# Retention by chunks of 128 tokens with a carried state, in plain fp32, two heads to a PSUM tile

## The chip, the cores and the metric

One core of a Trainium2 chip runs the kernel. The metric is the device time of one execution in microseconds, and of several executions the median. Engines: TensorE (PE, its weight loads PEld), VectorE (DVE), ScalarE (ACT), GpSimd (POOL) and SyncE (SP), whose queue issues all DMAs here.

## What is computed

Two transformer layers over 512 latent and 256 context tokens of width 1024: modulated norm, an input projection, four mixers side by side (a convolution, two attentions of 4 heads, a retention of 4 heads), an output projection and an MLP. The second layer gives no output for the context. The change is in the retention, which runs forward and backward (on the flipped sequence), for each head with keys of 32 and values of 64:

```python
def retention_chunked(q, k, v, log_gamma, s0, with_output):
    ...
    k_decay = jnp.exp(lg * (RET_CHUNK - 1.0 - idx))
    chunk_kv = jnp.einsum('bhnjd,bhnje->bhnde', kc * k_decay[:, None, :, None], vc)
    chunk_decay = jnp.exp(log_gamma * RET_CHUNK)[:, None, None]

    def step(s, kv_j):
        return s * chunk_decay + kv_j, s

    s_final, s_prev = lax.scan(step, s0, jnp.moveaxis(chunk_kv, 2, 0))
    ...
    decay = jnp.where(diff >= 0, jnp.exp(lg[:, :, None] * jnp.maximum(diff, 0.0)), 0.0)
    scores = jnp.einsum('bhnid,bhnjd->bhnij', qc, kc) * decay[:, None]
    inner = jnp.einsum('bhnij,bhnje->bhnie', scores, vc)
    q_decay = jnp.exp(lg * (idx + 1.0))
    cross = jnp.einsum('bhnid,bhnde->bhnie', qc * q_decay[:, None, :, None], s_prev)
    return (inner + cross).reshape(b, h, l, dv), s_final
```

The latent pass starts from the final state of the context pass.

## The kernel before

Most products are made of three fp32r products (`mm3`): each operand is split into an fp32r part and an fp32r rest (`split`: a cast on DVE or ACT, a subtraction on DVE or POOL). Some products are plain fp32, which the profile shows as two records each.

No instruction is issued as it is written. `Plan.record` (L195) notes each operation with the engines that may do it and a cost; `VS`, `VG` and `VSG` are operations that may go to DVE or ACT, DVE or POOL, or any of the three, while `V`, `S`, `G`, `T`, `D` fix the engine. `Plan.schedule` (L384) then runs a list scheduler on these costs: an operation's priority is its place in the recorded program, buffers in SBUF and PSUM are given out as it goes, and a flexible operation goes to the engine that would end it first (`worse`, L514). `Plan.issue` (L642) emits the order that results, so nearly all instructions have line L645, and all buffers of SBUF have the name m in the trace, PSUM tiles b and pp. Each engine executes its own list in order.

`order_of` (L672) sets in which sequence the parts of `mixing` are recorded: projections and their preparation first, then attention units (a head with 256 query rows: scores, softmax, transposes, product with V), and among the last of them the retention: `ret_in` (L1425) once, then a piece of `s_ret` (L1490) after each further unit. At the end stand `s_read` (L1591: transposes, norm, gate) and `out_proj` (L1645), whose results `add_gated` (L1638) adds.

The retention before: `s_ret` takes one head at a time, latent (512 rows) and context (256 rows) apart. For each key tile t of 128 it multiplies K and Q (a stack of 96 rows that holds the three products of the split) for all queries of the segment, then for each direction d copies the needed columns of the scores to SBUF on ACT (`D_ = (3, 3)`: both directions in both layers), multiplies them by a table of decays `tabs[d]` on DVE or POOL, and multiplies V by the result into `op_[d]`. The columns are 512, 384, 256 and 128 wide for the four key tiles (256 and 128 in the context):

```python
                    op_ = [psG(nm="of"), psG(nm="ob")]
...
                            if D_[l] >> d & 1:
                                sc_ = smt([128, 512], nm="sc")
                                S.copy(out=sc_[:, 0:n], in_=s[:, a:b])
                                VG.tensor_tensor(out=Dt[:, 0:n], in0=sc_[:, 0:n], in1=tabs[d][:, o:o + n], op=ALU.mult)
```

`R = (15, 3)` has a bit for each head of a layer in which V and the masked scores are multiplied as plain fp32 (`whole`: all heads of layer 0, heads 0 and 1 of layer 1); the others are split. The context's state enters as one term (`state` times `qdec`) over all 512 latent rows.

Of the kernel before, what the change touches and what calls it, by code (L numbers as in the profile page):

```python
# [22 lines left out]
R = (15, 3)  # L23
# [27 lines left out]
D_ = (3, 3)  # L51
# [648 lines left out]
def block_kernel(ctx: ExitStack, tc: tile.TileContext, x, c, cx, c_ctx, w_mod, b_mod, w_in, w_out,  # L700
# [307 lines left out]
    def mixing(l, ht, yt, todo, late=None):  # L1008
# [414 lines left out]
        vr, QK, qdec, state, oT = {}, [], [], [], []  # L1423

        def ret_in():  # L1425
            for pr in PAIRS:
                if R[l] == 15 and pr != CTX:
                    continue
                vr[pr] = bigt([128, 2, 4, 2, 64], F32R, nm="vr")
                u4 = ur[pr][:, :, 256:512].rearrange("p i (h d) -> p i h d", h=4)  # L1430
                for i in range(2):
                    split(vr[pr][:, i, :, 0], vr[pr][:, i, :, 1], u4[:, i])
            for qk in range(2):
                hl = [bigt([128, 512 if last else 768], F32R, nm="rqk") for _ in range(2)]
                for a, ts in ((0, LAT), (512, CTX)):
# [9 lines left out]
                    if a == 0 and qk == 0:  # L1445
                        for d in range(2):
                            qt = smt([128, 512], nm="qt")
                            D.dma_start(out=qt, in_=qexp[d].partition_broadcast(128))
                            S.activation(out=qt, in_=qt, func=AF.Exp, scale=lgc[:, l, d:d + 1])
                            VG.tensor_tensor(out=qt, in0=qt, in1=kf, op=ALU.mult)  # L1450
                            qdec.append(bigt([128, 2, 512], F32R, nm="qdec"))
                            split(qdec[d][:, 0], qdec[d][:, 1], qt)
# [10 lines left out]
            uk_ = ur[CTX][:, :, 128:256].rearrange("p i (h e) -> p i h e", h=4)  # L1463
            for d in range(2):
                kd = smt([128, 2, 4, 32], nm="kdec")
                VG.tensor_tensor(out=kd, in0=uk_, in1=kdt[:, :, d].unsqueeze(3).to_broadcast([128, 2, 4, 32]), op=ALU.mult)
                kw_ = smt([128, 2, 256], F32R, nm="kdec2")
                split(kw_[:, 0], kw_[:, 1], kd.rearrange("p i h e -> p (i h e)"))
                p = psG((128, 4, 64), nm="state")
                mm3(p, [(kw_[:, 0, i * 128:(i + 1) * 128], kw_[:, 1, i * 128:(i + 1) * 128], vr[CTX][:, i, :, 0],  # L1470
                         vr[CTX][:, i, :, 1]) for i in range(2)])
                sm = smt([128, 4, 64], nm="sm")
                V.tensor_tensor(out=sm, in0=p, in1=own.unsqueeze(2).to_broadcast([128, 4, 64]), op=ALU.mult)
                ss_ = bigt([128, 4, 2, 64], F32R, nm="state")
                split(ss_[:, :, 0], ss_[:, :, 1], sm)
                state.append(ss_)
# [13 lines left out]
        def s_ret():  # L1490
            for h in range(4):
                whole = bool(R[l] >> h & 1)
                tabs = []
                for d in range(2):
                    di = smt([128, 512], nm="di")
                    D.dma_start(out=di, in_=dist[d])
                    S.activation(out=di, in_=di, func=AF.Exp, scale=lgam[:, l * 8 + d * 4 + h:l * 8 + d * 4 + h + 1])
                    if d == 0:
                        G.affine_select(out=di[:, 0:128], in_=di[:, 0:128], pattern=[[1, 128]], compare_op=ALU.is_ge,
                                        fill=0.0, base=0, channel_multiplier=-1)  # L1500
                    else:
                        G.affine_select(out=di[:, 384:512], in_=di[:, 384:512], pattern=[[-1, 128]], compare_op=ALU.is_ge,
                                        fill=0.0, base=0, channel_multiplier=1)
                    tabs.append(di)
                st3 = []
                for qk in range(2):
                    t3 = a3t([96, 512 if last else 768], F32R, nm="st3")
                    for blk, hl in enumerate(((0, 1, 0), (0, 0, 1))[qk]):
                        D.dma_start(out=t3[32 * blk:32 * blk + 32].bitcast(F32),
                                    in_=QK[qk][hl][32 * h:32 * h + 32].bitcast(F32))  # L1510
                    st3.append(t3)
                for seg in segs:
                    Q4, K4 = [t3[:, (0, 512)[seg]:(512, 768)[seg]] for t3 in st3]
                    if seg == 0:
                        nq = 512
                        order = [0, 1, 2, 3]
                    else:
                        nq = 256
                        order = [4, 5]

                    def rng(d, t):

                        jt = t if seg == 0 else t - 4
                        if d == 0:
                            return 128 * jt, nq, 0
                        return 0, 128 * (jt + 1), 384 - 128 * jt

                    def inner(d, t, first, end):
                        a, b, o = rng(d, t)
                        if whole:  # L1530
# [20 lines left out]
                    for t in order:  # L1551
# [19 lines left out]
                        if seg == 0:  # L1571
                            for d in range(2):
                                inner(d, t, False, t == order[-1])
# [329 lines left out]
```

## Time and profile before

| | us |
|---|---|
| median of 3 runs (1842.2 to 1846.6) | 1844.59 |
| the profiled execution, its own time | 1847.59 |
| its span | 1845.9 |
| PE busy | 1706.8 (92%) |
| PEld busy | 1403.2 (76%) |
| DVE busy | 1355.0 (73%) |
| ACT busy | 684.3 (37%) |
| POOL busy | 394.6 (21%) |

The mixing of layer 0 lies at some 50 to 490 us, its projection and MLP until some 1100, the mixing of layer 1 until some 1450, its projection and MLP from there to the end. The mean granted clock of TensorE was 0.958 of full speed. Ends of matmuls are modelled, so PE's busy time is not PE at its peak. A row of a form gives the count, busy us, the mean ns of one, and the engine's idle time before them with what ended it.

### The profile page before, as it was taken

How to read it: one execution, taken by the hardware profiler on the slowest of the kernel's cores; microseconds unless marked ns; L12 is line 12 of the kernel's file. 1: busy time of each engine (PE TensorE's matmuls, PEld its weight loads, DVE VectorE, ACT ScalarE, POOL GpSimd, SP SyncE). 2: the span in 40 equal slices, each digit the busy share in tenths (PEclk: the TensorE clock that was granted, in tenths of full speed). 3: DMA queues.
4: the chain of work that ended last, by engine and by line, in shares of the span. 5: the costliest groups of instructions: out<-in, count | busy, mean ns of one | idle time of the engine just before them, and what ended most of it. 6: DMA issues, size and time to landing. Idle time of an engine off the chain costs nothing. (4 is left out here: it accounts for less than half of the span.)

```text
span 1845.9 us, 23213 instructions
## 1 busy us (share of the span) xinstructions
PE 1706.8 (92%) x8587; PEld 1403.2 (76%) x8587; DVE 1355.0 (73%) x2309; ACT 684.3 (37%) x1257; POOL 394.6 (21%) x358
## 2 busy tenths in 40 slices
PE   6995789989999999999999999959897989999998
PEld 4784568656788877888888889748765878888886
DVE  6889448888896788676765577974988776666665
ACT  5522027977443112111211135213997342222222
POOL 3318013651510010100100021120433421000001
PEclk9998799989999999999999999969997999999999
DMA  9220031534241434424421212110121533333331
GB/s 304 67 75 12 0 97 49 173 111 133 69 138 46 137 99 130 133 88 146 158 70 47 86 36 75 47 52 12 34 60 61 167 95 100 110 96 92 103 91 58
DMA packets 140641, 168.67 MB, mean 91 GB/s; under 512 B 7658, under 2 KB 93274, under 8 KB 140528
## 3 DMA queue, kind: packets, MB, share of 16 engines
q1 hardware_dynamic: 140528, 167.20, 29.5%
q8 instruction: 67, 1.10, 0.2%
q14 instruction: 46, 0.38, 0.1%
HBM read 161.14 MB, written 2.10 MB: 88 GB/s over the span
## 5 line engine op out<-in xcount | busy, mean ns | idle before, releaser
L645 PE MATMUL b<-m,m 128*128 128x512 f32 (+5 forms) x6452 | 1366.8, 370 | 49.6 <-DVE m L645 40.7
L645 PEld LDWEIGHTS b<-m,m 128*128 128x128 f32 (+2 forms) x6452 | 1123.2, 191 | 263.4 <-DVE m L645 39.4
L645 DVE TENSOR_TENSOR m<-m,m 128x512 fp32r<-128x512 f32 (+8 forms) x665 | 548.9, 844 | 138.0 <-PE b L645 79.9
L645 ACT CAST m<-m 128x1024 fp32r<-128x1024 f32 (+6 forms) x354 | 278.8, 808 | 666.2 <-PE b L645 462.8
L645 POOL TENSOR_TENSOR m<-m,m 128x1024 fp32r<-128x1024 f32 (+11 forms) x158 | 274.7, 1750 | 1087.7 <-ACT m L645 571.4
L645 DVE TENSOR_TENSOR m<-b,m 128x512 f32<-128x512 f32 (+12 forms) x346 | 208.6, 611 | 124.3 <-PE b L645 108.6
L645 PE MATMUL pp<-m,m 128*128 128x512 f32 (+6 forms) x848 | 206.0, 369 | 18.9 <-DVE m L645 9.7
L645 PEld LDWEIGHTS pp<-m,m 128*128 128x128 f32 (+2 forms) x848 | 148.1, 197 | 56.0 <-ACT m L645 15.8
L645 PE MATMUL b<-ident,m 128*128 128x128 f32 (+4 forms) x730 | 111.2, 280 | 27.5 <-DVE m L645 24.0
L645 ACT COPY m<-b 128x512 f32<-128x512 f32 (+7 forms) x176 | 82.8, 491 | 126.6 <-PE b L645 120.4
L645 DVE TENSOR_TENSOR m<-m 128x256 f32<-128x256 f32 (+1 forms) x104 | 63.4, 611 | 82.9 <-ACT m L645 82.4
L645 PEld LDWEIGHTS b<-ident,m 128*128 128x128 f32 (+4 forms) x730 | 84.7, 141 | 48.7 <-DVE m L645 28.2
L645 DVE SCALAR_TENSOR_TENSOR m<-m,sf,m 128x1024 f32<-128x1024 f32 x80 | 102.9, 1298 | 24.3 <-DMA m<-in_w_mod_dram 24.2
L645 DVE CAST m<-m 128x512 fp32r<-128x512 f32 (+4 forms) x163 | 77.8, 481 | 56.3 <-PE pp L645 31.7
L645 ACT ACTIVATE m<-b 128x512 f32<-128x512 f32 (+1 forms) x115 | 60.6, 529 | 149.0 <-PE b L645 140.6
L645 DVE SCALAR_TENSOR_TENSOR m<-m,cvw,m 128x783 f32<-128x783 f32 (+1 forms) x120 | 100.7, 887 | 0.6
L645 DVE TENSOR_REDUCE ty<-pp 128x1 f32<-128x768 f32 (+1 forms) x66 | 60.8, 932 | 9.2 <-PE pp L645 8.6
L645 ACT ACTIVATE m<-m 128x1024 f32<-128x1024 f32 (+4 forms) x65 | 42.0, 650 | 52.5 <-DVE m L645 42.9
L645 ACT ACTIVATE m<-pp,ty 128x768 f32<-128x768 f32 (+1 forms) x66 | 58.5, 888 | 4.4 <-PE b L645 3.0
L645 POOL TENSOR_TENSOR ty<-ty,mhalf 128x1 f32<-128x1 f32 (+4 forms) x47 | 57.3, 1225 | 2.3
L645 PE MATMUL pp<-ident,m 128*128 128x128 f32 (+3 forms) x252 | 41.6, 287 | 13.4 <-ACT m L645 7.5
L645 POOL TENSOR_SCALAR ty<-ty 128x2 f32<-128x2 f32 (+4 forms) x43 | 16.3, 380 | 166.3 <-ACT m L645 107.3
(112 smaller groups left out, 669.4 us busy)
## 6 DMA issues: line engine op xcount, KB each, us to landing
m<-in_mlp_w_dram SPq DMA_DIRECT2D x128, 512.0 KB
m<-in_w_mod_dram SPq DMA_DIRECT2D x96, 512.0 KB
m<-in_w_in_dram SPq DMA_DIRECT2D x32, 512.0 KB
m<-in_w_out_dram SPq DMA_DIRECT2D x16, 512.0 KB
m<-in_x_dram SPq DMA_DIRECT2D x8, 512.0 KB
m<-in_dist_dram SPq DMA_DIRECT2D x16, 256.0 KB
m<-in_w_in_dram SPq DMA_DIRECT2D x8, 416.0 KB
m<-m SPq DMA_DIRECT2D x24, 96.0 KB
```

The source lines that it names most:

```text
L645: op.fn(*[f(a) for a in op.args], **{k: f(a) for k, a in op.kw.items()})
```

## The change

`s_ret` now takes two heads, e = 0 and 1, and only the diagonal blocks of 128 by 128 of the latent scores: four 128-column products into one PSUM tile, one mask product for each direction, on DVE and straight from PSUM. What earlier chunks contribute comes from four states for each direction, which `ret_in` builds in a chain (context, then each chunk: decay K, multiply with V, keep each head's own block, multiply the last state by `g128` and add). V lies in `vz` with zeros beside it, so that each product writes all 128 rows of a tile of two heads and both heads add up in one PSUM tile; one eviction then serves two heads. The context segment keeps its full 256 columns. All these products are plain fp32; only the scores stay fp32r. The decay tables are 128 columns wide (256 in layer 0), and their exponents are loaded once for a layer. `order_of` is the same, but `s_ret` has 2 pieces where it had 8 and 4.

```diff
-            for pr in PAIRS:
-                if R[l] == 15 and pr != CTX:
-                    continue
-                vr[pr] = bigt([128, 2, 4, 2, 64], F32R, nm="vr")
+            for pr in opairs:
+                vz[pr] = bigt([128, 2, 4, 2, 64], nm="vz")
+                G.memset(vz[pr], 0.0)
                 u4 = ur[pr][:, :, 256:512].rearrange("p i (h d) -> p i h d", h=4)
-                for i in range(2):
-                    split(vr[pr][:, i, :, 0], vr[pr][:, i, :, 1], u4[:, i])
+                for k in range(2):
+                    VSG.copy(out=vz[pr][:, :, k::2, k], in_=u4[:, :, k::2])
...
-                            qt = smt([128, 512], nm="qt")
-                            D.dma_start(out=qt, in_=qexp[d].partition_broadcast(128))
+                            qt = smt([128, 128], nm="qt")
+                            D.dma_start(out=qt, in_=qexp[d, 384 * d:384 * d + 128].partition_broadcast(128))
                             S.activation(out=qt, in_=qt, func=AF.Exp, scale=lgc[:, l, d:d + 1])
-                            VG.tensor_tensor(out=qt, in0=qt, in1=kf, op=ALU.mult)
-                            qdec.append(bigt([128, 2, 512], F32R, nm="qdec"))
-                            split(qdec[d][:, 0], qdec[d][:, 1], qt)
+                            qdec.append(bigt([128, 512], nm="qdec"))
+                            VG.tensor_tensor(out=qdec[d].rearrange("p (c n) -> p c n", c=4),
+                                             in0=kf.rearrange("p (c n) -> p c n", c=4),
+                                             in1=qt.unsqueeze(1).to_broadcast([128, 4, 128]), op=ALU.mult)
...
+            g128 = cst([128, 2], f"g128{l}")
+            S.activation(out=g128, in_=lgc[:, l], func=AF.Exp, scale=128.0)
             for d in range(2):
...
+                for n in range(4):
...
+                        t = n - 1 if d == 0 else 4 - n
+                        kd = smt([128, 4, 32], nm="kdec")
+                        VG.tensor_tensor(out=kd, in0=tile_of(ur, t)[:, 128:256].rearrange("p (h e) -> p h e", h=4),
+                                         in1=kdt[:, 1 - d, d].unsqueeze(2).to_broadcast([128, 4, 32]), op=ALU.mult)
+                        items = [(kd, tile_of(ur, t)[:, 256:512])]
+                    p = psG((128, 4, 64), nm="state")
+                    for i, (a, b) in enumerate(items):
+                        T.matmul(p.rearrange("p h e -> p (h e)"), lhsT=a.rearrange("p h e -> p (h e)"), rhs=b,
+                                 start=i == 0, stop=i == len(items) - 1)
+                    st = bigt([128, 4, 64], nm="state")
+                    V.tensor_tensor(out=st, in0=p, in1=own.unsqueeze(2).to_broadcast([128, 4, 64]), op=ALU.mult)
+                    if n:
+                        V.scalar_tensor_tensor(out=st, in0=states[d][-1], scalar=g128[:, d:d + 1], in1=st,
+                                               op0=ALU.mult, op1=ALU.add)
+                    states[d].append(st)
...
         def s_ret():
-            for h in range(4):
...
+            tw = 128 if last else 256
+            di = [wkt([128, tw], nm="dist") for _ in range(2)]
+            D.dma_start(out=di[0], in_=dist[0, :, 0:tw])
+            D.dma_start(out=di[1], in_=dist[1, :, 512 - tw:512])
+            for e in range(2):
+                dts = []
+                for h in (2 * e, 2 * e + 1):
...
+                    s = psG(nm="sT")
+                    for c in range(4):
+                        cs = slice(c * 128, (c + 1) * 128)
+                        T.matmul(s[:, cs], lhsT=K3[:, cs], rhs=Q3[:, cs], start=True, stop=True)
+                    for d in range(2):
+                        dt = smt([128, 4, 128], nm="Dt")
+                        V.tensor_tensor(out=dt, in0=s.rearrange("p (c n) -> p c n", c=4),
+                                        in1=tabs[d][1].unsqueeze(1).to_broadcast([128, 4, 128]), op=ALU.mult)
+                        for c in range(4):
+                            dts.append((d, 0, h, c, c * 128, c * 128 + 128, dt[:, c]))
...
+                    for d in range(2):
+                        dt = smt([128, 384], nm="Dc")
+                        V.tensor_tensor(out=dt[:, 0:256], in0=s[:, d], in1=tabs[d][0], op=ALU.mult)
+                        V.tensor_tensor(out=dt[:, 256:384], in0=s[:, 1 - d, 128 - 128 * d:256 - 128 * d], in1=tabs[d][1],
+                                        op=ALU.mult)
...
                 for seg in segs:
...
+                    for d in range(2):
+                        o = psG(nm="oret")
                         if seg == 0:
...
+                            for c in range(4):
+                                cs = slice(c * 128, (c + 1) * 128)
+                                T.matmul(o[:, cs], lhsT=states[d][c][:, 2 * e:2 * e + 2].rearrange("p h e -> p (h e)"),
+                                         rhs=qdec[d][:, cs], start=c == 0, stop=False)
+                        mine = [x for x in dts if x[0] == d and x[1] == seg]
+                        for i, (_, _, h, t, a, b, m) in enumerate(mine):
+                            T.matmul(o[:, a:b], lhsT=tile_of(vz, t)[:, h].rearrange("p k e -> p (k e)"), rhs=m,
+                                     start=seg == 1 and i == 0, stop=i == len(mine) - 1)
+                        VS.copy(out=oT[d][e][seg], in_=o[:, 0:(512, 256)[seg]])
+                yield
```

The change also moves what the planner makes of the rest. Over the whole program PE has 7207 rows before and 7198 now, DVE 2124 and 2073, ACT 1103 and 1010, POOL 335 and 320, SP 415 and 404 (a row is an instruction or several equal ones in a row). Two places of it follow.

ACT in layer 0, before, in the middle of the retention (b and pp are PSUM tiles, m buffers of SBUF; copies of 512, 384, 256 and 128 columns are scores):

```order
L645 ACTIVATE m_7303,ty_3580<-b_3587,ty_3581 128x256
L645 CAST m_7316<-pp_7299 128x512
L645 COPY m_6627<-b_3587 128x512
L645 CAST m_7333<-pp_7300 128x512
L645 COPY m_7246<-b_3587 128x128
L645 COPY m_7137<-pp_7327 128x384
L645 COPY m_6627<-pp_7327 128x256
L645 COPY m_7351<-b_3586 128x256
L645 COPY m_7246<-b_3586 128x384
L645 COPY m_7355<-b_3587 128x128
```

and now, where the retention's tables are made (lgam holds the logarithms of the decays) and the softmax goes on:

```order
L643 ACTIVATE m_6305<-m_6227,lgam 128x256
L643 ACTIVATE m_6227<-m_6305,lgam 128x256
L643 CAST m_6777<-b_3426 64x256
L643 ACTIVATE m_3492<-m_6227,lgam 128x256
L643 ACTIVATE m_6784<-m_6305,lgam 128x256
L643 ACTIVATE m_6540<-m_6227,lgam 128x256
L643 ACTIVATE m_6540<-m_6305,lgam 128x256
L643 CAST m_5879<-pp_6678 64x512 x2
L643 COPY m_6589<-b_3424 64x256
L643 ACTIVATE m_6305,ty_3408<-pp_6903,ty_3407 128x768
L643 ACTIVATE m_6305<-m_6305,ty_3404 128x768
```

The copies of scores are gone from ACT, and six of the eight tables stand close together, each 256 wide.

DVE at the end of the mixing of layer 1, before (a reduction to 128x1 from pp is a softmax, one to 128x8 from m is the readout of the retention, the additions 64x512 and 64x256 from PSUM the last evictions of attention and retention):

```order
L645 TENSOR_REDUCE ty_3573<-pp_15551 128x1
L645 TENSOR_TENSOR m_15569<-m_15222,m_15333 128x1024
L645 TENSOR_TENSOR m_14879<-b_3588,m_14887 64x512
L645 RECIPROCAL ty_3564<-ty_3567 128x1
L645 TENSOR_TENSOR m_14879<-b_3585,m_14879 64x256
L645 TENSOR_TENSOR m_14929<-m_14879,m_14917 64x256
L645 TENSOR_TENSOR m_15616<-m_15264,m_15519 128x1024
L645 CAST m_15641<-m_14879 128x512
...
L645 TENSOR_REDUCE ty_3569<-m_14379 128x8
L645 TENSOR_REDUCE ty_3574<-m_14379 128x8
L645 TENSOR_REDUCE ty_3566<-m_14423 128x8
```

and now:

```order
L643 TENSOR_REDUCE ty_3410<-pp_15059 128x1
L643 TENSOR_TENSOR m_14198<-b_3427,ty_3404 128x512
L643 TENSOR_REDUCE ty_3408<-m_15017 128x8
L643 TENSOR_REDUCE ty_3403<-m_14023 128x8
L643 RECIPROCAL ty_3421<-ty_3413 128x1
L643 TENSOR_TENSOR m_14198<-pp_14947,m_14198 64x256
L643 TENSOR_TENSOR m_14023<-pp_14948,ty_3415 128x512
L643 TENSOR_REDUCE ty_3423<-pp_15107 128x1
```

The readout's reductions stood behind the last softmax; now the last two of its four, and with them all four, stand ahead of it.

## Rows read from the trace of the kernel before

**Rows 1.** Windows; columns PE, PEld, DVE, ACT, POOL busy, clock, DMA, GB/s.

```profile
285.00:380.00 95.00, 90.17 (x578) 69.89 (x577) 88.11 (x180) 86.64 (x173) 55.92 (x38) 0.98 0.41 128
380.00:490.00 110.00, 103.33 (x512) 68.49 (x512) 90.79 (x187) 74.78 (x165) 45.06 (x52) 0.92 0.32 99
850.00:900.00 50.00, 50.00 (x249) 42.46 (x248) 35.81 (x47) 7.32 (x10) 4.81 (x4) 1.00 0.31 97
1290.00:1390.00 100.00, 89.01 (x532) 68.89 (x531) 91.24 (x195) 92.49 (x198) 38.89 (x39) 0.98 0.20 59
1390.00:1448.00 58.00, 46.12 (x220) 36.97 (x219) 47.99 (x84) 36.35 (x66) 28.99 (x24) 0.82 0.18 64
```

**Rows 2.** Waits of DVE and ACT (380 to 490), PE (1390 to 1448): us, times, longest.

```profile
DVE m L645 <- PE b L645: 3.9, 5, 1.4
...
ACT m L645 <- PE b L645: 20.1, 14, 6.7
...
ACT m L645 <- DMA m<-in_dist_dram: 0.3, 1, 0.3
...
PE b L645 <- DVE m L645: 8.2, 5, 2.9
```

**Rows 3.** PE timeline in 403 to 414 and 1102 to 1104, one group by form.

```profile
405.34 0.43 PE L645 MATMUL pp<-m,m 128*64 128x128 f32 x2
407.84 0.65 PE L645 MATMUL b<-m,m 128*64 128x256 f32 x2
411.05 3.04 PE L645 MATMUL b<-m,m 128*128 128x256 f32 x20
...
1102.52 1.45 PE L645 MATMUL pp<-m,m 128*128 128x160 f32 x6
...
L645 PE MATMUL b<-m,m 128*128 128x512 f32 x4607 | 1072.2, 392 | 21.1 <-DVE m L645 13.5 <-ACT m L645 6.0 <-DVE modc L645 1.5
```

**Rows 4.** Groups by form on DVE, ACT and POOL, whole span.

```profile
L645 DVE TENSOR_TENSOR m<-m,m 128x512 f32<-128x512 f32 x191 | 143.6, 756 | 7.3 <-PE b L645 1.7 <-ACT m L645 0.7
L645 DVE TENSOR_TENSOR m<-m,m 128x384 f32<-128x384 f32 x20 | 13.1, 656 | 2.8 <-PE pp L645 1.5 <-PE b L645 1.0 <-ACT m L645 0.3
L645 DVE TENSOR_TENSOR m<-m,m 128x256 f32<-128x256 f32 x21 | 8.9, 440 | 1.4 <-POOL m L645 1.1 <-PE b L645 0.3
L645 DVE TENSOR_TENSOR m<-m,m 128x128 f32<-128x128 f32 x22 | 7.3, 337 | 0.2
L645 DVE TENSOR_TENSOR m<-b,m 128x512 f32<-128x512 f32 x180 | 122.8, 687 | 107.4 <-PE b L645 105.7
L645 DVE CAST m<-m 128x512 fp32r<-128x512 f32 x98 | 44.3, 455 | 5.0 <-ACT m L645 2.3 <-PE b L645 0.3
L645 DVE SCALAR_TENSOR_TENSOR m<-m,cvw,m 128x512 f32<-128x512 f32 x60 | 41.9, 746 | 0.3
L645 ACT COPY m<-b 128x512 f32<-128x512 f32 x78 | 44.5, 593 | 91.9 <-PE b L645 91.1 <-PE pp L645 0.4
L645 ACT COPY m<-b 128x384 f32<-128x384 f32 x17 | 8.4, 493 | 7.2 <-PE b L645 7.2
L645 ACT COPY m<-b 128x256 f32<-128x256 f32 x20 | 7.6, 378 | 10.5 <-PE b L645 9.1 <-DVE m L645 1.2
L645 ACT COPY m<-b 128x128 f32<-128x128 f32 x13 | 3.5, 280 | 0.0
L645 ACT ACTIVATE m<-m,lgam 128x512 f32<-128x512 f32 x16 | 11.1, 722 | 0.4 <-DMA m<-in_dist_dram 0.3
L645 ACT ACTIVATE m<-m 128x256 f32<-128x256 f32 x12 | 5.0, 416 | 0.2
L645 ACT ACTIVATE m<-m 128x128 f32<-128x128 f32 x14 | 4.2, 303 | 0.1
L645 POOL MEMSET m<- 128x1024 f32 x10 | 9.3, 952 | 50.2 <-issue 28.2 <-DVE m L645 14.3 <-PE b L645 7.6
```

**Rows 5.** Group by form on DVE in 380 to 490.

```profile
L645 DVE TENSOR_TENSOR m<-b,own 128x256 f32<-128x256 f32 x1 | 0.4, 414 | 0.0
```

More of the change, by code (lines that the diff above doesn't have):

```diff
@@ L22 @@
 F = (0, 0)
-R = (15, 3)
 Q = (1, 1)
@@ L50 @@
 J = (0, 7)
-D_ = (3, 3)
 NCUT = 2
@@ L1420, in mixing @@
                 units.append(Unit(gqa_prep(h, pr, whole), h, 4, 2, pr, whole))
-        vr, QK, qdec, state, oT = {}, [], [], [], []
+        vz, QK, qdec, states, oT = {}, [], [], [[], []], []
         def ret_in():
-            for pr in PAIRS:
-                if R[l] == 15 and pr != CTX:
-                    continue
-                vr[pr] = bigt([128, 2, 4, 2, 64], F32R, nm="vr")
+            for pr in opairs:
+                vz[pr] = bigt([128, 2, 4, 2, 64], nm="vz")
+                G.memset(vz[pr], 0.0)
                 u4 = ur[pr][:, :, 256:512].rearrange("p i (h d) -> p i h d", h=4)
-                for i in range(2):
-                    split(vr[pr][:, i, :, 0], vr[pr][:, i, :, 1], u4[:, i])
+                for k in range(2):
+                    VSG.copy(out=vz[pr][:, :, k::2, k], in_=u4[:, :, k::2])
             for qk in range(2):
@@ L1462, in ret_in @@
             V.tensor_scalar(out=kdt, in0=kdt, scalar1=32.0 ** -0.5, scalar2=None, op0=ALU.mult)
-            uk_ = ur[CTX][:, :, 128:256].rearrange("p i (h e) -> p i h e", h=4)
+            g128 = cst([128, 2], f"g128{l}")
+            S.activation(out=g128, in_=lgc[:, l], func=AF.Exp, scale=128.0)
             for d in range(2):
[L1465 to L1476, printed above, removed]
@@ new lines, in ret_in @@
+                for n in range(4):
+                    if n == 0:
+                        kd = smt([128, 2, 4, 32], nm="kdec")
+                        uk_ = ur[CTX][:, :, 128:256].rearrange("p i (h e) -> p i h e", h=4)
+                        VG.tensor_tensor(out=kd, in0=uk_, in1=kdt[:, :, d].unsqueeze(3).to_broadcast([128, 2, 4, 32]),
+                                         op=ALU.mult)
+                        items = [(kd[:, i], ur[CTX][:, i, 256:512]) for i in range(2)]
+                    else:
+                        t = n - 1 if d == 0 else 4 - n
[13 more added lines that the diff above has]
+                    states[d].append(st)
@@ L1477, in ret_in @@
+            states[1].reverse()
             oT.extend([[[bigt([128, (512, 256)[s]], nm="oT") for s in segs] for _ in range(2)] for _ in range(2)])
```

116 lines of the change are left out of this document (25 added, 91 removed).

## The prediction

> **What bounds the kernel now.** I read the stages first, in the view of windows [rows 1]. In the MLP of layer 0 (850 to 900) PE is busy all 50 us and the two other engines idle a good part: there PE is the bound. In the mixing it is the other way round. In 285 to 380 DVE is busy 88.11 of 95 us and ACT 86.64; in 1290 to 1390 it is 91.24 and 92.49 of 100. PE looks busy there too (90.17, 89.01), but its ends are modelled, its weight loads fill only 70% of the time, and in the last stretch, 1390 to 1448, it falls to 46.12 of 58 with a granted clock of 0.82. The retention runs in 380 to 490 and 1390 to 1448, where DVE still does 90.79 of 110 and 47.99 of 58.
>
> Then the waits [rows 2]. In 380 to 490 ACT waits 20.1 us for PE; DVE idles 19.2 us in all (110 less 90.79), in small waits of which 3.9 us are for PE; and in 1390 to 1448 PE waits 8.2 us for DVE. So in the mixing DVE and ACT hand work to each other in a nearly full pipeline, and PE follows. The question is what the change takes from DVE and ACT, and the PE saving comes second.
>
> **PE.** A plain fp32 product is two records, and alone takes 0.43 us for 128 and 0.65 us for 256 columns [rows 3], so some 0.21 us for each block of 128 columns in a chain. Before, a head needs 26 such blocks in layer 0 (20 latent, 6 context); now 14, and 4 for its share of the carried states: 8 blocks less, 32 in all, 6.8 us. The three-product cross terms also go: 24 products of 512 columns at 0.23 us (busy over count in [rows 3]: 1072.2 us for 4607), 5.5 us. The carried states add 20 blocks against 12 narrow products: 2.8 us more. The scores fall from 16 products of 512 to 16 of 128 columns. No row shows that shape. A 160-column fp32r product takes 0.24 us (1.45 us for 6), more than a 256-column one (3.04 us for 20, 0.15 us); below, a quarter of 0.23 is 0.06. I take 0.21, the nearer row, so the scores save next to nothing. Sum for layer 0: about 9.5 us less; for layer 1, without context rows and with the two split heads, about 5. The Trainium skill, "FP8 and Floating Point Precision", "TensorE Precision Notes", separates reduced fp32 from true fp32 with its four passes; by a single pass in proportion to columns the scores would cost 0.06 us each and PE would save 2.4 us a layer more. The 160-column row speaks against it. The time hardly depends on it, since PE is not what ends the waits here.
>
> **DVE, ACT and POOL, which carry the sum** (durations from [rows 4] unless said).
> Removed in layer 0:
> - Score copies on ACT: per head and direction 512, 384, 256, 128 columns latent and 256, 128 context, at 0.593, 0.493, 0.378 and 0.280 us: 4.81 us a head, **19.2 us**.
> - Mask products on DVE or POOL at 0.756, 0.656, 0.44 and 0.337 us: **23.7 us**.
> - Evictions of half-height outputs, 8 at 0.593 and 8 at 0.378: 7.8 us. Tables, 8 exponentials at 0.722: 5.8 us.
> - Decayed queries, 2 times 0.722 + 0.756 + 0.455 + 0.756: 5.4 us. Context V, decayed K and states: 6 pairs of a cast (0.455) and a 256-wide product (0.44), and 4 single products: 7.1 us.
> Sum: 69 us.
> Added in layer 0:
> - Mask products straight from PSUM, on DVE alone: per head 2 of 512 at 0.687, and 2 of 256 and 2 of 128 at an estimated 0.42 and 0.28 (the 512 row scaled, a fixed part kept): **11.1 us**.
> - Tables at 0.416: 3.3 us. Evictions, half as many at full height: 3.9 us. Padded V: 3 fills at 0.952 on POOL and 6 copies at the cast's 0.455: 5.6 us. Decayed queries, an exponential at 0.303 and a product at 0.756 twice: 2.1 us.
> - State chain: 8 decays of K (2 at 0.44, 6 at 0.337), 8 masks by owner at 0.414 [rows 5], 6 multiply-adds. The form of the last is absent; between a 256-wide product (0.44) and a 512-wide multiply-add (0.746) I take 0.5. Together 9.2 us.
> Sum: 35 us. **Net 34 us less** on three engines.
> Layer 1 in the same way, with latent rows only: copies 14.0, masks 17.5, evictions 7.5, tables 5.8, the hi/lo split of the masked scores of heads 2 and 3 and of all V 18.7 (4 times 1.14 of cast, by columns, and 2.19 of subtraction; 6 pairs), the rest 10.8: 74 us; added 25 (masks 5.5). **Net 49 us less.** Some flexible operations move between engines, so what matters is what the plan gives each. In the new order ACT has 93 rows fewer, DVE 51, POOL 15. Adding up DVE's instructions of each order at the durations of their forms, up to the first gated addition of the output projection, DVE loses only 5 us in layer 0 but some 22 in layer 1; most of layer 0's relief is ACT's and POOL's.
>
> DMA: 16 loads of 256 KB for the distance tables become 4 smaller ones, and the SP queue gets shorter. ACT waited 0.3 us for them [rows 2], so I count nothing. The queue positions of the projection weights hardly move.
>
> **What of it reaches the time.** If DVE alone bounds the stage, layer 0 gains 5 us and layer 1 22. If the relief is shared evenly by DVE and ACT, 17 and 24. Layer 0: I take 10, since DVE's 19.2 us of idle time [rows 1] sit in the retention and shrink when a score needs one hop fewer. Layer 1: I take 21, near the DVE end, because DVE was full through 1290 to 1390. There the plan also puts the readout ahead of the last softmax, so its products are not left for the tail. What is late next is that last softmax chain in layer 1, and the PE-bound projection in layer 0. Sum 31 us. The profiled execution took 1847.59 us (span 1845.9), so 1816.6; the median of the runs is 3.0 below it, so **1813.6 us**.
>
> **Rivals.**
> - *Even sharing, and the clock recovers.* ACT's relief counts as much as DVE's: 17 + 24 = 41, and the low clock in 1390 to 1448 (0.82, so PE lost up to 10 us there) goes in part: 46 us, 1798.6. For it: ACT as full as DVE in 285 to 380. Against: the DVE count of layer 0.
> - *Only the fixed chain counts.* The order was made for costs that differ from the measured ones, and new waits open where DVE must read scores from PSUM: layer 0 gains nothing, layer 1 half (11): 1834. For it: DVE idles 17% of 380 to 490 though work is at hand on every engine.
> - *The clock falls.* Where PE does less, the granted clock was lower: 0.92 and 0.82 against 1.00 in the MLP [rows 1]. The Trainium skill, "TensorE: Matmul & The Clock Gate", Part 1, says that activity opens the clock and idling closes it between 1.2 and 2.4 GHz; the two rows agree. As a mechanism here: 0.08 of 110 and 0.18 of 58 us of clock missing mean 18 and 21 us at half rate, 39 us, which cost PE 19 us of work. Were the half-rate time doubled by thinner PE work, 19 of the 31 us come back: 1833.
> - *DVE stands behind PSUM (slower).* The mask products are now DVE's alone and stand in its in-order queue behind score matmuls; softmax reductions queue behind them. ACT took that wait before: 20.1 us in 14 waits, 1.4 us each [rows 2]. There are 24 such products in layer 0 and 8 in layer 1; at 1.4 us each, 46 us minus 31 gained: 15 slower, 1860. It decides above 1.0 us a product. Against: DVE's own waits for PE are 3.9 us in 5 times there, 0.8 us each, and the planner puts other ready work in between.
> - *It does not reach the time.* All that goes was hidden under PE, as PE's 94% in 380 to 490 would have it: 1844.6. Against: PE waits for DVE.
>
> **How the numbers follow.** Forecast (gain 24 to 38) 0.56; even sharing 0.13; only the chain 0.15; clock 0.07; DVE behind PSUM 0.05; no effect 0.04. The range reaches from the even-sharing case to the two smaller gains, with 1 us of spread between runs at either end (1842.2 to 1846.6 before): 1798 to 1835. No change means within 0.2%, 3.7 us, about what a measurement can tell. Faster 0.91, same 0.04, slower 0.05.
>
> **What would show it.** Right: in the mixing windows ACT's share falls clearly below DVE's; layer 1's mixing ends some 20 us earlier relative to its start, layer 0's some 10; the MLP stretches keep their length; PE has about 15 us less work; 128-column scores show 0.2 us each. Wrong: DVE idle behind PE in the retention (the slower rival), granted clock under 0.8 over the whole retention, or a layer 0 that gains as much as layer 1.

## The result, and the profile after

The changed kernel takes 1796.67 us (median of 4 executions, 1796.0 to 1801.06), beside 1843.39 us (1838.34 to 1846.6) for the kernel before in the same comparison: ratio 0.9754, 95% interval 0.9726 to 0.9782. That is 46.7 us less, where 31 were forecast; 1796.67 lies 1.3 us below the low end of the range. The profiled execution took 1797.3 us. One execution of the kernel before, in a later comparison, ran in a slow state (3408 us) and is left out of every figure.

The first part of the profile of the changed kernel, busy time and share of the span:

```profile
span 1795.6 us, 23051 instructions
PE 1662.4 (93%) x8623; PEld 1395.0 (78%) x8623; DVE 1321.9 (74%) x2257; ACT 641.6 (36%) x1166; POOL 377.8 (21%) x338
```

Against the table of before, DVE lost 33 us, ACT 43, POOL 17 and PE 44. The windows that answer to [rows 1], moved by the shift of their stage (columns as there):

```profile
282.00:377.00 95.00, 91.81 (x590) 70.64 (x589) 86.52 (x185) 87.85 (x179) 56.34 (x40) 0.98 0.38 116
377.00:476.00 99.00, 87.22 (x546) 74.05 (x544) 83.83 (x178) 57.38 (x117) 39.98 (x39) 0.97 0.34 105
834.00:884.00 50.00, 50.00 (x248) 42.36 (x247) 36.15 (x47) 7.32 (x10) 4.88 (x4) 1.00 0.33 100
1267.00:1367.00 100.00, 89.51 (x625) 77.90 (x624) 95.85 (x196) 88.50 (x181) 39.20 (x41) 1.00 0.20 56
1367.00:1401.00 34.00, 31.82 (x175) 26.37 (x174) 28.77 (x49) 19.64 (x38) 19.48 (x16) 1.00 0.30 99
```

Layer 0's first stretch and the MLP are as they were. In its retention (377 to 476) ACT fell from 68% to 58% of the window while DVE stayed at 83 to 85%. In layer 1 DVE is fuller than before (95.85 of 100 against 91.24), the granted clock is 1.00 to the end, and the thin stretch at the end (PE 46.12 of 58 us, clock 0.82) is now 34 us long with PE busy for 31.82. The waits that answer to [rows 2], in 377 to 476 (engine, what it waited for: us, times, longest):

```profile
ACT m L643 <- PE b L643: 20.5, 13, 4.5
...
DVE m L643 <- PE b L643: 3.2, 1, 3.2
```

They are much as they were. With the waits of the softmax reductions and for PE's other tiles counted, DVE waited 11.8 us for PE (9.5 in 380 to 490 before): it does not stand behind PSUM, although it now reads all scores there.

To see each layer whole, the span is cut at the first softmax reduction of each layer. But for a few preparations, both pieces hold the same parts of the program in every kernel: the first is layer 0's mixing with its MLP and the change of layers, the second is layer 1 from there to the end. The two windows before:

```profile
177.80:1203.70 1025.90, 974.94 (x4988) 802.42 (x4988) 753.34 (x1273) 357.93 (x674) 190.09 (x180) 0.96 0.30 93
1203.70:1845.90 642.20, 587.59 (x2836) 483.39 (x2836) 458.34 (x742) 252.89 (x440) 126.17 (x107) 0.95 0.27 81
```

and after:

```profile
175.10:1180.90 1005.80, 949.42 (x5004) 799.55 (x5004) 743.47 (x1260) 339.49 (x629) 193.49 (x170) 0.97 0.31 93
1180.90:1795.60 614.70, 571.02 (x2856) 479.81 (x2856) 437.16 (x703) 228.62 (x392) 105.20 (x97) 0.97 0.27 81
```

Layer 0's piece is 20.1 us shorter, layer 1's 27.5; the remaining 2.7 us lie ahead of the first softmax (177.8 us before, 175.1 after), where GpSimd and ACT already have a few changed instructions. They need not be the change's doing: in the run without the split below, whose instructions are those of before up to there, the first softmax starts at 175.4. DVE lost 9.9 us in the first piece and 21.2 in the second. These windows, taken in every run, are the measure below.

### The profile page after: what moved, and what is told of

It is laid out like the page before. It is cut to its first block, busy times and chain, and to the rows that moved or that the text cites. A ratio compares the mean times of both kernels' runs of the same rounds, so it can differ in the third digit from the quotient of the medians.

```text
span 1795.6 us, 23051 instructions
## 1 busy us (share of the span) xinstructions
PE 1662.4 (93%) x8623; PEld 1395.0 (78%) x8623; DVE 1321.9 (74%) x2257; ACT 641.6 (36%) x1166; POOL 377.8 (21%) x338
## 5 line engine op out<-in xcount | busy, mean ns | idle before, releaser
L643 PE MATMUL b<-m,m 128*128 128x512 f32 (+5 forms) x6460 | 1334.2, 366 | 34.9 <-DVE m L643 27.3
L643 PEld LDWEIGHTS b<-m,m 128*128 128x128 f32 (+1 forms) x6460 | 1119.5, 191 | 232.0 <-DVE m L643 22.4
L643 DVE TENSOR_TENSOR m<-m,m 128x512 f32<-128x512 f32 (+10 forms) x582 | 510.2, 893 | 125.3 <-PE b L643 79.6
L643 ACT CAST m<-m 128x1024 fp32r<-128x1024 f32 (+5 forms) x332 | 267.3, 821 | 669.9 <-PE b L643 481.9
L643 POOL TENSOR_TENSOR m<-m,m 128x1024 fp32r<-128x1024 f32 (+6 forms) x130 | 245.9, 1899 | 1083.3 <-ACT m L643 619.8
L643 PEld LDWEIGHTS pp<-m,m 128*128 128x128 f32 (+1 forms) x860 | 144.1, 192 | 49.9 <-ACT m L643 17.2
L643 PE MATMUL b<-ident,m 128*128 128x128 f32 (+4 forms) x762 | 112.5, 276 | 30.4 <-DVE m L643 27.3
L643 DVE TENSOR_TENSOR m<-m 128x512 f32<-128x512 f32 (+1 forms) x104 | 61.0, 588 | 82.2 <-ACT m L643 81.3
L643 ACT COPY m<-b 128x512 f32<-128x512 f32 (+5 forms) x132 | 65.4, 509 | 124.7 <-PE b L643 120.5
L643 DVE CAST m<-m 128x512 fp32r<-128x512 f32 (+3 forms) x149 | 75.8, 511 | 25.3 <-DMA m<-in_w_mod_dram 9.8
L643 ACT ACTIVATE m<-pp,ty 128x768 f32<-128x768 f32 (+1 forms) x65 | 58.1, 895 | 10.5 <-DVE ty L643 8.9
L643 DVE TENSOR_SCALAR m<-m,ty 128x512 f32<-128x512 f32 (+3 forms) x94 | 43.0, 494 | 9.9 <-POOL ty L643 9.5
```

What stands on the lines that cost most here:

```text
L643: op.fn(*[f(a) for a in op.args], **{k: f(a) for k, a in op.kw.items()})
```

## The experiments

Times are medians, ratios are to the kernel before in the same comparison. The two pieces and DVE's and ACT's busy time in layer 1's piece come from one profiled execution of each; for layer 0's piece the three profiles with its old code (before, layer 1 alone, no split) gave 1025.9, 1017.0 and 1022.2, so a single profile is good to some 5 us there. The four runs that undo a part of the change were compared with the kernel before, and not with the change itself; where their medians are set beside the change's, two comparisons are crossed, and the ratios are the safer measure.

| kernel | us | ratio (95%) | layer 0 piece | layer 1 piece | DVE, ACT in it |
|---|---|---|---|---|---|
| before | 1843.4 | 1 | 1025.9 | 642.2 | 458.3, 252.9 |
| after | 1796.7 | 0.9754 (0.9726 to 0.9782) | 1005.8 | 614.7 | 437.2, 228.6 |
| layer 0 alone | 1831.5 | 0.9931 (0.991 to 0.9951) | 1011.3 | 644.9 | 460.4, 253.2 |
| layer 1 alone | 1808.7 | 0.9799 (0.9774 to 0.9824) | 1017.0 | 610.2 | 437.1, 229.0 |
| no split | 1829.3 | 0.992 (0.9895 to 0.9945) | 1022.2 | 626.9 | 447.9, 245.3 |
| no copies | 1840.2 | 0.9976 (0.9952 to 1.0001) | 1026.3 | 638.9 | 452.9, 246.7 |
| neither | 1831.1 | 0.9929 (0.9905 to 0.9954) | 1023.9 | 629.5 | 441.8, 235.5 |
| PE added | 1867.7 | 1.0127 (1.0078 to 1.0176) | 1036.6 | 652.5 | 458.4, 253.5 |
| DVE added | 1868.7 | 1.013 (1.0086 to 1.0174) | 1036.1 | 654.8 | 471.7, 252.9 |
| ACT added | 1867.5 | 1.0113 (1.008 to 1.0147) | 1032.2 | 656.9 | 459.7, 266.3 |
| after, by chunk | 1805.6 | 0.9781 (0.974 to 0.9822) | 1015.0 | 620.7 | 441.8, 228.7 |
| after, single heads | 1801.8 | 0.9775 (0.9724 to 0.9826) | 1005.0 | 610.1 | 434.8, 233.4 |
| after, with copies | 1814.3 | 0.9834 (0.9789 to 0.9879) | 1002.8 | 627.4 | 444.9, 230.9 |
| after, late | 1803.1 | 0.9769 (0.9726 to 0.9811) | 995.3 | 622.8 | 438.7, 227.7 |

**The layers apart.** Both forms stand in one file, and a table chooses for each layer (the first run has (1, 0), the second (0, 1)):

```diff
+CH = (1, 0)
...
+        ret_in, s_ret = (ret_in_new, s_ret_new) if CH[l] else (ret_in_old, s_ret_old)
```

> The chunked form in layer 0 alone; layer 1 keeps the old form. Theory A (relief of DVE and ACT ends the mixing, each layer keeps its own gain, and the 6.5 us at the change of layers belong to layer 0's work): 12 us in the mixing of layer 0 and 2 to 7 us up to layer 1, so 14 to 19 us less than before, about 1826; the first softmax of layer 1 comes 12 to 20 us earlier and the stretch from there to the end keeps its 643 us. Theory B (PE's clock: less PE work of one layer costs or gives time in the other): the stretch after the first softmax of layer 1 changes by more than 3 us though its program is unchanged. Theory C (luck of the planned order at the layer change): the change of layers keeps its low clock (near 0.5 in about 14 us) and only 9 to 12 us are gained, 1831 to 1835.

> The chunked form in layer 1 alone; layer 0 keeps the old form. Theory A: the 28 us of layer 1's mixing are gained whole, 25 to 30 us less than before, about 1816, and the change of layers keeps its 6.5 us. Theory B (half of the gain hangs on a clock that only the full change keeps up): under 20 us gained, with a granted clock under 0.9 in the last 50 us of layer 1's mixing. Theory C (the gain at the layer change is luck of the order): the 6.5 us come here or are lost here without any change in layer 0's code; the total differs from 28 us by some 6 either way.

By their ratios layer 0 gains 12.7 us (9 to 17) and layer 1 37 us (32 to 42), together 50 beside the 46.7 of the change: they add up within their intervals. In layer 0's run the unchanged piece of layer 1 moved by 2.7 us, less than theory B asked for. Between A and C it doesn't decide: layer 1 begins 19.1 us earlier, as A had it, but the low clock at the change of layers stays, as C had it (0.89 in 1070 to 1130, 0.89 before), and the gain lies between theirs. Layer 1 alone gained more than A and B said; C's 28 and some 6 lies within its interval, and the clock at its change of layers is 1.00.

In the run with layer 1 alone, the piece of layer 0 was 8.9 us shorter in the profile. The next run shows that this need not be the change's doing.

**The split taken away.** The kernel before with all heads of layer 1 plain fp32:

```diff
-R = (15, 3)
+R = (15, 15)
```

> The kernel before with heads 2 and 3 of layer 1 as plain fp32 too, so that the hi/lo split of their masked scores and of V is gone and nothing else. By the forecast's sum this takes 18.7 us of DVE, ACT and POOL work away. Theory A (work of DVE and ACT, shared): 6 to 10 us faster. Theory B (in the last 50 us of layer 1's mixing PE stands behind the serial chain copy, mask, split, product, and its clock falls there): 10 us or more, with the low clock (0.79 in the last 48 us) going to 0.9 or above. Theory C (the chunking itself, not the split, is what counts): under 4 us.

It gained 14.8 us (10 to 19); in the profile, the piece of layer 1 is 15.3 shorter: theory B's size. Of the tail of the mixing before, the thinnest 20 us,

```profile
1400.00:1420.00 20.00, 11.75 (x52) 9.13 (x50) 17.91 (x33) 11.85 (x22) 9.10 (x7) 0.67 0.01 1
```

and the 20 us of this run that lie about as close ahead of the last softmax reduction (at 1423.3 us before, 1406.3 here):

```profile
1385.00:1405.00 20.00, 19.26 (x86) 10.81 (x87) 17.82 (x35) 17.87 (x39) 4.77 (x5) 1.00 0.39 120
```

PE no longer starves, and the clock stays up. DVE lost 10.4 us in the piece. Taken one for one, two thirds of the gain are DVE's work, and the rest goes with the tail; no run separates the two.

Up to 1306 us this kernel issues the very instructions of the kernel before, in the same order, on PE, DVE, ACT and POOL. Yet its layer 1 begins 6 us earlier. Its window around the change of layers,

```profile
1070.00:1130.00 60.00, 58.24 (x325) 52.53 (x324) 48.09 (x99) 29.29 (x67) 18.70 (x28) 1.00 0.21 61
```

and the same window of the kernel before:

```profile
1070.00:1130.00 60.00, 58.45 (x291) 52.83 (x290) 42.70 (x84) 25.45 (x54) 17.56 (x24) 0.89 0.17 46
```

The same program once had the clock and once not. So such a gain at the change of layers can be the chance of one execution. The profile of after has one too, with the clock at 1.00 in 1070 to 1130: between a DMA of the MLP's weights at 1017 us of before and the convolution's run of taps in layer 1 (at 1157), its lead grows from 16.2 to 22.8 us. There the instructions differ, so how much of it is chance is not shown.

**The copies taken away, alone and with the split.** The mask products of the old form straight from PSUM; the second run has `R = (15, 15)` as well:

```diff
-D_ = (3, 3)
+D_ = (0, 0)
```

> The kernel before with the mask products straight from PSUM on DVE, so that the 33 us of score copies on ACT are gone and all mask products (some 41 us) are DVE's. Theory A with DVE as the bound: slower by 2 to 15 us, since the products that POOL did move to DVE. Theory A with ACT as an equal bound: faster by 5 to 15 us. Rival of the forecast (DVE stands behind PSUM): slower by 20 us or more, with waits of DVE for PE of over 1 us at each of the 64 products.

> The kernel before without score copies (mask products on DVE straight from PSUM) and with all heads of layer 1 plain fp32, but not chunked: full rows of up to 512 columns, one head at a time. If the copies and the split were all of the gain in layer 1: about 1800, 45 us less than before. If they add up as they did alone: 4 + 15 = 19 us less, and the rest of the whole change's 47 us (some 28) belongs to the chunking and the pairs of heads. If without the split the copies matter more (ACT then the only hop between PE and PE): 25 to 35 us less.

Alone it gains 4.4 us (none to 9), with the split removed 13.1 us (8 to 18), no more than the split's removal by itself. ACT had 20.5 us less in all by the first part of the profile (684.3 before, 663.8), DVE 1.9 (1355.0, 1353.1): ACT's relief hardly counts. DVE did not get fuller, since the planner gave other work of DVE away, and it did not stand behind PSUM either: from the first to the last softmax its waits for PE came to 48.3 us in layer 0 and 28.9 in layer 1, beside 48.9 and 26.6 before. Some 30 us of the whole change were then still to be explained.

**Some 30 us added to one engine.** The order of instructions stays that of the kernel before; only at the issue are chosen instructions repeated. The three runs differ in `REP`: {("score", "T"): 5}, {("mask", "V"): 2} and {("copy", "S"): 2}.

```diff
-            op.fn(*[f(a) for a in op.args], **{k: f(a) for k, a in op.kw.items()})
+            for _ in range(REP.get((op.kind, op.on), 1)):
+                op.fn(*[f(a) for a in op.args], **{k: f(a) for k, a in op.kw.items()})
```

> The kernel before, in its own order of instructions, with each score product of the retention issued five times in a row (the same result): 32.9 us of PE work more (128 products of 512 columns at 0.227 us, 32 of 256 at 0.12), 18.4 in layer 0 and 14.5 in layer 1. If PE does not bound the mixing (the forecast): 0 to 8 us slower. If PE, or a chain through it, is the bound: 20 to 33 us slower. If thin PE work is what lowers the granted clock: fewer half-clock stretches in the retention, and less than 0 to 5 us slower.

> The kernel before, in its own order of instructions, with each mask product that stands on DVE issued twice (the same result): 30.7 us of DVE work more in both layers together (57 instructions). If DVE is the bound of the mixing (the forecast's first end): 20 to 31 us slower, layer 1 by its whole share. If the relief is shared by DVE and ACT: 10 to 20 us. If PE or only the fixed order bounds: under 8 us.

> The kernel before, in its own order of instructions, with each score copy on ACT issued twice (the same result): 33.2 us of ACT work more (80 copies; 19.2 in layer 0, 14.0 in layer 1). If DVE alone is the bound: under 8 us slower. If DVE and ACT share it: 10 to 20 us. If ACT is the bound in layer 0's retention (where it was seen waiting 20 us for PE): under 5 us there, and more in layer 1.

The profiles show 27.3 us more on PE, 27.0 on DVE and 31.2 on ACT, somewhat less than was worked out. By the ratios these cost 23 us (14 to 32), 24 (16 to 32) and 21 (15 to 27). No single engine bounds the retention in the fixed order. That score, copy, mask and product form one chain, in which work added to any link delays what stands in order behind it by two thirds or more, fits all three. DVE's cost is what its being the bound would give, PE's and ACT's are more than that theory gave them. It doesn't follow that work taken away counts as much, since the planner then makes another order: the copies' removal showed that it doesn't.

**The change with one part undone.** Scores handed over chunk by chunk, then heads one at a time, then the copies back, then the retention recorded later:

```diff
-                    s = psG(nm="sT")
                     for c in range(4):
                         cs = slice(c * 128, (c + 1) * 128)
-                        T.matmul(s[:, cs], lhsT=K3[:, cs], rhs=Q3[:, cs], start=True, stop=True)
+                        s = psG((128, 128), nm="sT")
+                        T.matmul(s, lhsT=K3[:, cs], rhs=Q3[:, cs], start=True, stop=True)
+                        for d in range(2):
+                            dt = smt([128, 128], nm="Dt")
+                            V.tensor_tensor(out=dt, in0=s, in1=tabs[d][1], op=ALU.mult)
```

> The changed kernel with its latent scores handed over chunk by chunk: each 128-column score product in a PSUM tile of its own, and a mask product of 128 columns for each direction, 32 instead of 8 in each layer, the same columns. DVE gets some 3.5 us more in each layer by fixed parts (32 of 0.28 us against 8 of 0.687). Theory of hand-offs (the layer 1 gain that the split and the copies do not explain, some 12 us, comes from four scores handed over at once): 8 to 15 us of layer 1's gain come back, 1805 to 1815. Theory of work (engines' sums count at about 0.7): 4 to 6 us slower than the change, 1801 to 1803. Order only: within 3 us of 1796.7.

Its executions (1802.2 to 1813.3) lie above all of the change's (1796.0 to 1801.1); the medians differ by 8.9 us, the ratios by 5, within their intervals. In the profile, which is the slowest execution, layer 1 gave back 6.0 us for 4.6 us more of DVE, layer 0 9.2 for 6.3. The ratio is that of the theory of work, the median that of hand-offs; but layer 1 gave back less than the 8 to 15 us that hand-offs asked for there, so that four scores at once save 12 us in layer 1 is not borne out.

```diff
+                        for hh in (2 * e, 2 * e + 1):
...
+                                T.matmul(o[0:64, a:b], lhsT=tile_of(ur, t)[:, 256 + h * 64:320 + h * 64], rhs=m,
+                                         start=seg == 1 and i == 0, stop=i == len(mine) - 1)
```

> The changed kernel without the pairs of heads: V unpadded (no fills and copies), each head's products into 64 rows of a PSUM tile of its own, one eviction for each head as before. Removed: 5.6 us of fills and copies; added: 3.9 us of evictions in layer 0 and some 2.4 in layer 1. Theory of work: within 3 us of 1796.7. Theory of hand-offs (twice the PSUM tiles and evictions at the end of each pair): 3 to 10 us slower.

1794.6 to 1812.3, median 5 us above the change (4 by the ratios): the executions overlap, and nothing can be told. Pairing two heads in a PSUM tile carries little of the gain, if any.

```diff
-                        V.tensor_tensor(out=dt, in0=s.rearrange("p (c n) -> p c n", c=4),
+                        sc_ = smt([128, 512], nm="sc")
+                        S.copy(out=sc_, in_=s)
+                        VG.tensor_tensor(out=dt, in0=sc_.rearrange("p (c n) -> p c n", c=4),
```

> The changed kernel with the score copies on ACT back, at the chunked sizes: 8 copies of 512 columns in each layer and 24 smaller ones in layer 0 (some 4.7 us of ACT in layer 1 and 12 in layer 0), and mask products free to go to POOL. Theory of work at 0.7: 3 us slower in layer 1 and up to 8 in layer 0, 1800 to 1808. If direct reading by DVE costs as much as the copy saves (as it nearly did alone in the old form, 4 us gained by 33 us of ACT): within 4 us of 1796.7.

1806.1 to 1819.3, median 17.6 us above the change (15 by the ratios, whose intervals lie apart): beyond both theories. The profiled execution was the fastest, and has 12.7 us of the loss in layer 1, where 4.7 us of copies came back. Its piece of layer 1:

```profile
1177.00:1804.40 627.40, 577.54 (x2856) 484.75 (x2856) 444.90 (x705) 230.87 (x395) 106.17 (x100) 0.96 0.26 79
```

ACT has 2.3 us more than after, but DVE 7.7 us more, though six of the eight mask products of layer 1 went to GpSimd. These are the six:

```profile
1316.57 3.09 POOL L643 TENSOR_TENSOR m<-m,m 128x512 f32<-128x512 f32 x2 [2.34 <-ACT m L643]
1319.83 1.27 POOL L643 TENSOR_TENSOR m<-m,m 128x512 f32<-128x512 f32 x1 [0.17 <-ACT m L643]
...
1327.78 1.51 POOL L643 TENSOR_TENSOR m<-m,m 128x512 f32<-128x512 f32 x1 [4.18 <-ACT m L643]
...
1330.52 2.62 POOL L643 TENSOR_TENSOR m<-m,m 128x512 f32<-128x512 f32 x2
```

So direct reading is worth little in the old form (4.4 us) and some 12 us in layer 1 here, and in single profiles chunks without direct reading gain no more in layer 1 than the removal of the split (627.4 against 626.9): the two parts seem to pay only together. The section below on the hardware names a part of what DVE loses with the copies.

```diff
-o0 = (1, 0, 0, 9)
-o1 = (1, 1, 0, 6)
+o0 = (1, 0, 0, 3)
+o1 = (1, 1, 0, 4)
```

> The changed kernel with the retention recorded later, so that its last piece stands where the last piece of the old form stood (after the last attention unit but one in layer 0, and with two units to go in layer 1); nothing else is changed. If the change gains because its two pieces end earlier in the recorded order, and the readout is not left for the tail: 5 to 15 us slower, 1802 to 1812, with the last softmax of layer 1 later. If the place does not matter: within 3 us of 1796.7.

1794.4 to 1805.6: unclear as a whole, 6.4 us above by medians, 3 by the ratios. In the one profile layer 0 was 10.5 us shorter and layer 1 8.1 longer. That the early place helps layer 1 agrees with it, and for layer 0 the late place may be better; late in layer 0 alone wasn't tried.

## Why the prediction was right in sign, and short in size

**What held.** The mixing itself came out near the forecast. From the start of the first to the start of the last softmax reduction of a layer, layer 0's fell from 289.0 to 280.8 us and layer 1's from 219.6 to 195.3: 8.2 and 24.3, where 10 and 21 were forecast. The two stretches before:

```profile
177.82:466.86 289.04, 252.17 (x1308) 183.67 (x1309) 208.25 (x459) 169.66 (x347) 94.51 (x88) 0.91 0.29 90
1203.66:1423.29 219.63, 178.93 (x956) 143.35 (x957) 167.11 (x374) 139.19 (x277) 60.95 (x62) 0.90 0.14 40
```

and after:

```profile
175.14:455.95 280.81, 240.43 (x1373) 191.50 (x1374) 201.48 (x461) 158.04 (x314) 96.34 (x86) 0.93 0.28 85
1180.85:1376.16 195.31, 164.74 (x990) 141.88 (x991) 148.50 (x333) 120.15 (x236) 56.00 (x60) 0.93 0.16 47
```

Layer 1's stretch repeats: 220.6 us with its old code (the run with layer 0 alone), 195.0 with the new (layer 1 alone). Layer 0's old code scatters by some 4 us either way (285.1, 293.5), so its 8.2 is rough. DVE's relief was forecast as 5 us in layer 0 and some 22 in layer 1. In layer 1's piece 21.2 went. Over the runs without added work, layer 1's piece follows DVE's busy time in it, from 458 and 642 us down to 435 and 610, at about 1.3 us a us (a straight line through the 11 profiles leaves some 4 us). DVE's waits for PSUM in layer 0's retention were 3.9 us before and 3.2 after, the MLP kept its pace, ACT's share fell below DVE's in layer 0's retention (not ahead of it, in 282 to 377). The slower rival (DVE behind PSUM) is out, and so is the rival of no effect.

**The step that failed: "What of it reaches the time".** It gave layer 1 21 us and layer 0 10, and nothing else. DVE's relief, if it counts one for one, explains 9.9 + 21.2 = 31 us. That rate is an assumption: the run with work added to DVE bears it out (27 us cost 24), the two without copies in the old form don't (below). This is the forecast's sum, but layer 0's 10 came from another source than the idle time that I named: from the first to the last softmax DVE's idle time went from 80.8 to 79.3 us only, and DVE itself lost twice what I had counted, most of it in stretched instructions that went (below). So that layer 0's number agreed is in part luck. Most of the excess lies outside the mixing: from layer 0's last softmax to layer 1's first one the profile is 11.9 us shorter than before, and the run without the split, with the very instructions of before, 8.1, behind a mixing of layer 0 that was 4.5 us longer. Two things were left at zero:

- The clock. I called its recovery a rival at 0.13, and its fall another. It rose: 0.960 in the mean over 33 executions of before in the comparisons, 0.968 over the four of after. At 1843 and 1797 us that is 148 and 114 us at the half rate, 34 us less. Among the 33 executions of the one program the time rises with the half-rate time, by 0.33 us for one us (1830.7 to 1852.0 us, correlation 0.80). So the clock is worth an estimated 11 us: 42 of 46.7. This is a correlation within one program; no run moved the clock alone.
- PE's work. "PE is not what ends the waits" is refuted for the fixed order: 27 us more of it cost 23. PE's busy time fell by 44 us, or by 26 with its busy time at the half rate counted as half, where 15 were forecast. How much of the last 5 us is PE's lighter load can't be told from the spread of the runs.

The rival of even sharing gave 46 us and 1798.6, nearest to the result, but by the wrong road: it let ACT's relief count as DVE's, and the run without copies speaks against that. Its clock term was the right one, and too small. In single runs the sum isn't exact: the two runs without copies in the old form gained 8 and 9 us less in layer 1 than DVE's relief one for one and the clock at 0.33 together give. Why is open.

**A mis-sized row.** I priced a 128-column score at 0.21 us by the 160-column row of [rows 3], 0.24 us each. That row stood where the clock was at half rate, as this window of before shows:

```profile
1102.00:1108.00 6.00, 6.00 (x28) 5.60 (x28) 3.98 (x12) 4.89 (x9) 3.08 (x4) 0.54 0.14 42
```

The timeline of PE after has the same 160-column products (nine in 1.13 us) and the scores (four in 0.64 and 0.56 us, the end of the last included):

```profile
405.61 0.64 PE L643 MATMUL b<-m,m 96*128 96x128 f32 x4
...
1088.03 1.13 PE L643 MATMUL b<-m,m 128*128 128x160 f32 x9
...
1326.28 0.56 PE L643 MATMUL pp<-m,m 96*128 96x128 f32 x4
```

So 0.13 us for 160 columns and at most 0.16 for 128: the expected 0.2 was not shown. In 16 products a layer the slip is worth 1 us. The lesson is to look at the clock of the stretch a price is read from.

## What to carry to other kernels

Where a stage is a chain over several engines, follow the busy time of the one that is nearly full (here DVE, at 1.3 us a us) and add the clock that comes back when PE no longer starves at its end; relief of a neighbour that waits anyway (ACT) was worth little, though work added to it cost nearly as much as on DVE. Check whether an edit moves an operand from SBUF to PSUM: beside GpSimd a DVE product of 512 columns took 1.29 us with both inputs in SBUF and 0.68 with one in PSUM. Before a price is taken from a row, look at the granted clock of its window, and before a gain is credited to an edit, look whether a run with the same instructions there shows it too.

## What the runs showed of the hardware that I had not expected

DVE and GpSimd block each other when both read SBUF, and I costed both by mean rows. In the tail of layer 1 before, the split of the masked scores shows it; GpSimd in 1405 to 1418, start and us:

```profile
1410.11 7.22 POOL L645 TENSOR_TENSOR m<-m,m 128x512 fp32r<-128x512 f32 x4 [3.61 <-ACT m L645]
```

DVE beside it:

```profile
1408.45 2.36 DVE L645 TENSOR_TENSOR m<-m,m 128x512 fp32r<-128x512 f32 x6 [0.63 <-ACT m L645]
1410.73 1.56 DVE L645 CAST m<-m 128x256 fp32r<-128x256 f32 x2
1412.21 5.73 DVE L645 TENSOR_TENSOR m<-m,m 128x256 fp32r<-128x256 f32 x4
1417.87 0.48 DVE L645 CAST m<-m 128x384 fp32r<-128x384 f32 x2
1418.27 1.35 DVE L645 TENSOR_TENSOR m<-m,m 128x384 fp32r<-128x384 f32 x3
```

and PE, which waited for it:

```profile
1413.76 0.79 PE L645 MATMUL b<-m,m 128*128 128x256 f32 x2 [2.56 <-DVE m L645]
```

Six products of 128 to 512 columns take 2.36 us while GpSimd is idle for most of them; four of 128 to 384 columns take 5.73 while it runs. Counted over the whole span of before, products of 512 columns with both inputs in SBUF take 0.689 us where no GpSimd product lies beside them (306) and 1.288 where one lies beside them for over half their time (26). With one input in PSUM it is 0.687 (191) and 0.679 (53): no difference. It goes the other way too. The depthwise taps of the convolution run back to back on DVE until 165, and GpSimd's products of 128 columns, timeline of before:

```profile
135.28 31.12 POOL L645 TENSOR_TENSOR m<-m,m 128x128 fp32r<-128x128 f32 x3 [20.18 <-ACT m L645]
...
166.78 0.45 POOL L645 TENSOR_TENSOR m<-m,m 128x128 fp32r<-128x128 f32 x1
```

take 0.45 us alone; the first of the three took 30.3 of their 31.12 us, until DVE's run of taps ended at 165. The Trainium skill, "SBUF — State Buffer", section "Who interferes with whom", says that a DVE instruction with two SBUF inputs contends with a GpSimd instruction that reads SBUF, and that one with at most one SBUF input doesn't, outside DVE's two-port modes, which casts among others can enter. The products agree with it. The casts, with one SBUF input each, show that the exception matters: of the two at 1410.73 the first took 0.28 us and the second, beside GpSimd, 1.18. Which mode they ran in no row shows.

Summing what DVE's instructions took beyond the lower quartile of their own operation, tiles and shape (where over 0.15 us), from the first to the last softmax of a layer: before 8.3 us in layer 0 and 11.3 in layer 1; after 0.4 and 4.1; with the copies back 2.9 and 10.2. Each of these instructions lies beside one of GpSimd. So 6 of the 7.7 us that DVE gained in layer 1 with the copies back are of this kind. They are not in the mask products: two of the eight ran on DVE, at 0.68 us each, and the other six on GpSimd. What got longer were DVE's other instructions, the longest a multiply-add of the carried states (0.47 us at 1346, 3.42 here), shown with GpSimd beside it:

```profile
1342.82 3.42 DVE L643 SCALAR_TENSOR_TENSOR m<-m,g,m 128x256 f32<-128x256 f32 x1
...
1341.57 4.39 POOL L643 TENSOR_TENSOR m<-m,m 64x256 fp32r<-64x256 f32 x4
```

Whether this is why the two parts pay only together stays open. In the old form without copies and split the same sum is 3.0 us in layer 1, less than after, and yet that run gained only 13 us; no run took GpSimd's products away to show their share by itself.
